# Reading each weight block in an order that alternates between its two halves: a float32r decoder layer on one core

## The chip, the core and the metric

The kernel runs on one core of a Trainium2 chip. The metric is the device time of one execution in microseconds (us); the time before is the median of 3 runs. The engines are named as in the profile: PE is TensorE (PEld its weight loads), DVE is VectorE, ACT is ScalarE, POOL is GpSimd, SP is SyncE, which here only issues DMAs.

## The reference

One layer of a decoder over 256 tokens of width 2048, in float32. Three attention branches of 4, 6 and 6 heads share one input projection; each branch is projected, gated and added; then an output projection with residual, and a SwiGLU feed-forward of width 5632 with residual.

```python
h = rmsnorm(x, g_mix)
proj = h @ w_in                      # 2048 -> 3*2048 (q, k, v) + 3*2048 (gates)
...
merged = (gates[:, :, 0] * (flat(o_a) @ w_branch[:ea])
          + gates[:, :, 1] * (flat(o_b) @ w_branch[ea:eb])
          + gates[:, :, 2] * (flat(o_c) @ w_branch[eb:]))
x = x + merged @ w_out
h2 = rmsnorm(x, g_ffn)
gu = h2 @ w_gu                       # 2048 -> 2*5632
x = x + (jax.nn.silu(gu[..., :D_FF]) * gu[..., D_FF:]) @ w_down
```

Nearly all the arithmetic is in the five matrices w_in, w_branch, w_out, w_gu and w_down.

## The kernel before

**Precision.** A float32 factor is kept as two float32r parts, high and low: `split` (line 104) lets ScalarE copy the value into a float32r tile (the high part) and VectorE subtract that from the value (the low part). A product of two such factors is three matmuls: high by high, high by low, low by high (`product`, lines 160 to 164). In each, a 128 x 128 piece of the activations (`h`, `hs`, `o`, `m`, `h2`, `a`) is the stationary operand, and a 128 x 512 piece of a weight is the moving one; the result goes to a 128 x 512 bank in PSUM.

**Tiling.** On the host, `by_blocks` (line 1083) lays each matrix out in blocks of 256 rows by 512 columns, so that one DMA of 512 KB brings a tile of 128 partitions x 2 x 512 words (`w_raw`, or `g_raw` where blocks are added to one another first). The tile is split into `w_hi` and `w_lo` (line 105), 128 x 1024 words in one instruction each, and every half of 512 is then the moving operand of products with both blocks of 128 tokens.

**Stages.** In order: the values, queries and keys, and gates from w_in, with the attention of earlier groups woven in by generators that advance a step after each weight block; the branch projections (w_branch) with the gates; the output projection (w_out); the feed-forward's first matrix (w_gu); its second (w_down). `project` (line 142) handles a group of 512 columns in the plain way. `project_pair` (line 320) and `down_pair` (line 974) take two groups at once, and for part of the rows use seven products in place of eight, with sums of activations and sums of weight blocks (`u`, lines 305 and 316). The first four row blocks of the first group go through an order written by hand (lines 500 to 506) beside the loading of x. All these ways end in the same matmuls of 128 x 512: lines 162, 163, 164, and 500, 503, 506.

**Other matmuls.** Transposes (line 184) and the attention (lines 632 to 712) use plain float32; eight matmuls on zeros (line 380) fill TensorE's time at the start.

**Order.** A scheduler sets the order of instructions on each engine, but for those that are pinned. SP issues all weight DMAs, into tiles of which 4 (`w_raw`) or 4 to 6 (`g_raw`) are there at a time; POOL issues the gates, the residual and the spilled activations.

Of the kernel before, what the change touches and what calls it, by code (L numbers as in the profile page):

```python
# [17 lines left out]
P = 128  # L18
# [10 lines left out]
NB = 512  # L29
# [25 lines left out]
def hybrid_block(ctx: ExitStack, tc: tile.TileContext, x, g_mix, w_in, q_gain, k_gain, w_branch, w_out,  # L55
                 g_ffn, w_gu, w_down, rel_bias, onehot, extra, out):
    nc = tc.nc
# [36 lines left out]
    def banks():  # L94

        turn.reverse()
        return [acc.tile([P, NB], F32, name=turn[1]) for _ in range(2)]
# [44 lines left out]
    def project(acts, k0, w, row0, nk, col0, ps=None, done=0, there=(), last=1):  # L142


        ps = ps or banks()
        held = []
        for k, w_hi, w_lo in weights(w, row0, done, nk, col0, there):
            if k:
                advance(stages)
            if k % 2 == 0 and k:  # L150
                advance(slow_stages)
            held.append((k, w_hi, w_lo))
            if k < nk - last or k == nk - 1:
                for t in range(NT):
                    for kk, hi, lo in held:
                        product(ps[t], *acts.plain(t, k0 + kk), hi, lo, kk == 0, kk == nk - 1)
                held = []
        return ps

    def product(ps, ah, al, wh, wl, start=False, stop=False):  # L160
        how = dict(skip_group_check=True)
        nc.tensor.matmul(ps, ah, wh, start=start, stop=False, **how)  # L162
        nc.tensor.matmul(ps, ah, wl, start=False, stop=False, **how)  # L163
        nc.tensor.matmul(ps, al, wh, start=False, stop=stop, **how)  # L164
# [155 lines left out]
    def project_pair(acts, w, colA, colB, begun=None, nxt=None):  # L320
# [7 lines left out]
        def form(ps, f, srcs, start, stop, split=False):  # L328
            for i, c in enumerate(acts.wc):
                wh, wl = srcs[i] if split else parts(srcs[i])  # L330
                for j in range(2):
                    product(ps, *acts.form(f, c, j), wh[:, j], wl[:, j], start and i + j == 0,
                            stop and i + j == len(acts.wc))

        def rest(n, k, p0, p1, start=False, stop=False):
            wh, wl = parts(load(w, k, cols[n]))
            for t, ps in ((1, p1), (0, p0)):
                for j in range(2):
                    product(ps, *acts.plain(t, k + j), wh[:, j], wl[:, j], bool(start and t == 1 and j == 0), stop and j == 1)
# [53 lines left out]
    h = Columns(p1, "h", KT)  # L393
# [58 lines left out]
    for k in (4, 6):  # L452
# [6 lines left out]
    columns = {c: [o_raw[:, 4 * i + 2 * t:4 * i + 2 * t + 2, :].rearrange("p h (a q) -> p (h a) q", a=2)  # L459
                   for t in range(NT)] for i, c in enumerate(WC)}  # L460
# [26 lines left out]
    ps0 = banks()  # L487
    his, los = ([wpool.tile([P, 2, NB], F32R, name=f"w_{n}") for _ in range(2)] for n in ("hi", "lo"))
    W_HI, W_LO = ([t[k // 2][:, k % 2] for k in range(4)] for t in (his, los))
    RAW = [raws[k // 2][:, k % 2] for k in range(4)]  # L490
    how = dict(skip_group_check=True, stop=False)
# [5 lines left out]
        nc.vector.tensor_sub(W_LO[k], RAW[k], W_HI[k].bitcast(F32))  # L497

    def high_high(t, k):
        nc.tensor.matmul(ps0[t], h.plain(t, k)[0], W_HI[k], start=k == 0, **how)  # L500

    def high_low(t, k):
        nc.tensor.matmul(ps0[t], h.plain(t, k)[0], W_LO[k], start=False, **how)

    def low_high(t, k):
        nc.tensor.matmul(ps0[t], h.plain(t, k)[1], W_HI[k], start=False, **how)

    with tc.manual_schedule(engines={mybir.EngineType.PE, mybir.EngineType.DVE, mybir.EngineType.Activation}):
        high(0)
        first_columns(0, 0, 2)  # L510
        first_columns(0, 2, 2)
        idle(3)
        high_high(0, 0)
        first_columns(1, 0, 4, False)
        low(0)
        high(1)
        high_high(0, 1)
        low_part(0)
        high_low(0, 0)
        low_high(0, 0)  # L520
        first_columns(1, 0, 4, True)
        low(1)
        low_high(0, 1)
        high_low(0, 1)
        turned = [transpose4(xs[1][0])]
        high_high(1, 0)
        high_high(1, 1)
        high_low(1, 0)
        high(2)
        low_part(1)  # L530
        high_low(1, 1)
        low_high(1, 0)
        low_high(1, 1)
        low(2)
# [412 lines left out]
    a = Chunks(None, "a", NF // 4, WD, False)  # L947
# [135 lines left out]
def by_blocks(w):  # L1083

    rows, columns = w.shape[1:]
    w = w[0].reshape(rows // (2 * P), 2, P, columns // NB, NB)
    return np.ascontiguousarray(w.transpose(3, 0, 2, 1, 4))


# [18 lines left out]
```

## Time and profile before

| | before |
|---|---|
| median of 3 runs | 1432.87 us (1432.37 to 1435.72) |
| span of the profiled execution | 1432.0 us |
| PE busy | 1422.3 us, 99%, 6404 matmuls |
| PEld busy | 1172.0 us, 82% |
| DVE busy | 1196.6 us, 84% |
| ACT busy | 881.7 us, 62% |
| moved by DMA | 310.09 MB, 217 GB/s |

The profile is one execution. Its span runs from the first to the last instruction; the median lies 0.9 us above it. A row of a group gives line, engine, operation, output <- inputs, shapes and count, then busy us and the mean ns of one, then the idle time of the engine before them and what ended it. Matmuls are pipelined, so their durations overlap, and the pace is the distance between starts. PEclk is the granted TensorE clock in tenths.

### The profile page before, as it was taken

The numbers are of one execution on the slowest core, as the hardware profiler recorded it, in microseconds if no ns is written. First come the engines' busy times: TensorE is split into PE (matmuls) and PEld (weight loads), VectorE is DVE, ScalarE is ACT, GpSimd is POOL, SyncE is SP. The second block draws the span as 40 slices with busy tenths as digits, with TensorE's granted clock in tenths as the row PEclk, the third lists the DMA queues.
The fourth block names the chain that finished last, engine by engine and source line by source line (L and its number), as shares of the span: only waits on it lengthen the run. The fifth ranks groups of instructions, "written<-read, shape, count | busy, mean of one in ns | idle before, by whom it ended". The sixth has DMA issues, their size and how long they took to land. (4 is left out here: it accounts for less than half of the span.)

```text
span 1432.0 us, 17773 instructions
## 1 busy us (share of the span) xinstructions
PE 1422.3 (99%) x6404; PEld 1172.0 (82%) x6404; DVE 1196.6 (84%) x1262; ACT 881.7 (62%) x1140; POOL 72.9 (5%) x133
## 2 busy tenths in 40 slices
PE   9999999999999999999999999999999999999998
PEld 7888888888888888888888888888888888788887
DVE  7888787857999887776689999999999998886775
ACT  7667876766766665444456666666666666554453
POOL 1000000000000002100100000000000010100000
PEclk9999999999999999999999999999999999999999
DMA  8763547464656758876786657566665666767552
GB/s 269 262 221 123 216 120 250 123 219 173 217 202 239 255 195 297 273 218 217 226 293 222 225 205 256 213 222 233 222 214 192 233 207 232 253 233 237 190 169 97
DMA packets 88168, 310.09 MB, mean 217 GB/s; under 512 B 10672, under 2 KB 12288, under 8 KB 88080
## 3 DMA queue, kind: packets, MB, share of 16 engines
q1 hardware_dynamic: 76896, 275.29, 56.1%
q0 software_dynamic: 10000, 32.62, 6.6%
q8 instruction: 50, 0.82, 0.2%
q10 hardware_dynamic: 1184, 1.06, 0.2%
q14 instruction: 38, 0.31, 0.1%
HBM read 292.65 MB, written 16.27 MB: 216 GB/s over the span
## 5 line engine op out<-in xcount | busy, mean ns | idle before, releaser
L105 DVE TENSOR_TENSOR w_lo<-w_raw,w_hi 128x1024 fp32r<-128x1024 f32 x334 | 406.3, 1222 | 90.8 <-ACT w_hi L105 87.3
L105 ACT CAST w_hi<-w_raw 128x1024 fp32r<-128x1024 f32 x334 | 349.2, 1052 | 165.2 <-PE qs L164 69.5
L105 ACT CAST w_hi<-g_raw 128x1024 fp32r<-128x1024 f32 x184 | 192.7, 1053 | 121.4 <-PE ps L164 41.2
L105 DVE TENSOR_TENSOR w_lo<-g_raw,w_hi 128x1024 fp32r<-128x1024 f32 x184 | 219.9, 1221 | 39.2 <-ACT w_hi L105 38.5
L105 ACT CAST w_hi<-u 128x1024 fp32r<-128x1024 f32 x138 | 145.1, 1054 | 136.0 <-DVE u L305 64.4
L105 DVE TENSOR_TENSOR w_lo<-u,w_hi 128x1024 fp32r<-128x1024 f32 x138 | 166.5, 1222 | 37.1 <-ACT w_hi L105 35.7
L163 PE MATMUL ps<-w_lo,h_hi 128*128 128x512 f32 x360 | 140.9, 391 | 0.0
L164 PE MATMUL ps<-w_hi,h_lo 128*128 128x512 f32 x360 | 140.5, 390 | 0.0
L162 PE MATMUL ps<-w_hi,h_hi 128*128 128x512 f32 x360 | 137.4, 392 | 0.0
L163 PE MATMUL qs<-w_lo,h_hi 128*128 128x512 f32 x332 | 129.9, 391 | 0.8 <-DVE w_lo L105 0.8
L164 PE MATMUL qs<-w_hi,h_lo 128*128 128x512 f32 x332 | 129.5, 390 | 0.0
L162 PE MATMUL qs<-w_hi,h_hi 128*128 128x512 f32 x332 | 126.6, 391 | 0.0
L305 DVE TENSOR_TENSOR u<-u,g_raw 128x1024 f32<-128x1024 f32 x80 | 94.4, 1219 | 0.0
L164 PEld LDWEIGHTS ps<-w_hi,h_lo 128*128 128x128 f32 x360 | 67.6, 188 | 14.3 <-DVE h_lo L105 0.3
L163 PEld LDWEIGHTS ps<-w_lo,h_hi 128*128 128x128 f32 x360 | 67.6, 188 | 13.6
L162 PEld LDWEIGHTS ps<-w_hi,h_hi 128*128 128x128 f32 x360 | 67.5, 188 | 13.7
L163 PEld LDWEIGHTS qs<-w_lo,h_hi 128*128 128x128 f32 x332 | 62.4, 188 | 13.9 <-DVE w_lo L105 1.2
L164 PEld LDWEIGHTS qs<-w_hi,h_lo 128*128 128x128 f32 x332 | 62.3, 188 | 13.5 <-issue 0.6
L162 PEld LDWEIGHTS qs<-w_hi,h_hi 128*128 128x128 f32 x332 | 62.3, 188 | 12.7
L316 DVE TENSOR_TENSOR u<-g_raw 128x1024 f32<-128x1024 f32 x40 | 48.8, 1220 | 17.5 <-DMA g_raw<-in_w_in 14.8
L162 PE MATMUL v<-w_hi,h_hi 128*128 128x512 f32 x120 | 47.5, 396 | 0.2 <-ACT w_hi L105 0.2
L305 DVE TENSOR_TENSOR g_raw<-g_raw 128x1024 f32<-128x1024 f32 x40 | 47.1, 1219 | 0.0
(397 smaller groups left out, 2934.6 us busy)
## 6 DMA issues: line engine op xcount, KB each, us to landing
w_raw<-in_w_in SPq DMA_DIRECT2D x118, 512.0 KB, 4.6
g_raw<-in_w_gu SPq DMA_DIRECT2D x88, 512.0 KB, 5.1
w_raw<-in_w_gu SPq DMA_DIRECT2D x88, 512.0 KB, 5.9
g_raw<-in_w_in SPq DMA_DIRECT2D x72, 512.0 KB, 5.6
w_raw<-in_w_down SPq DMA_DIRECT2D x64, 512.0 KB, 4.4
w_raw<-in_w_branch SPq DMA_DIRECT2D x32, 512.0 KB, 4.5
w_raw<-in_w_out SPq DMA_DIRECT2D x32, 512.0 KB, 4.1
g_raw<-in_w_down SPq DMA_DIRECT2D x24, 512.0 KB, 4.6
```

The costliest lines, as they stand in the source:

```text
L105: for op in nc.scalar.copy(hi, src), nc.vector.tensor_sub(lo, src, hi.bitcast(F32)):
L162: nc.tensor.matmul(ps, ah, wh, start=start, stop=False, **how)
L163: nc.tensor.matmul(ps, ah, wl, start=False, stop=False, **how)
L164: nc.tensor.matmul(ps, al, wh, start=False, stop=stop, **how)
L305: tc.keep_in_program_order(nc.vector.tensor_add(d, d, a))
L316: nc.vector.tensor_add(d, a, b)
```

## The change

The host lays out each row of 512 columns of a block with its 256 even columns first and its 256 odd columns behind them. The two parts of every weight tile keep that layout. Each matmul that reads such a part as its moving operand reads it through the view `woven`: for each b of 256, the word b of the first half, then the word b of the second. So the 512 results stand in PSUM in the natural order of the columns, as before. The sums of weight blocks are formed elementwise in the new layout. The lists of instructions of each engine, with shapes and order, are the same before and after.

```diff
+    def woven(w):
+
+        return w.rearrange("p (a b) -> p b a", a=2)
+
     def product(ps, ah, al, wh, wl, start=False, stop=False):
         how = dict(skip_group_check=True)
+        wh, wl = woven(wh), woven(wl)
         nc.tensor.matmul(ps, ah, wh, start=start, stop=False, **how)
         nc.tensor.matmul(ps, ah, wl, start=False, stop=False, **how)
         nc.tensor.matmul(ps, al, wh, start=False, stop=stop, **how)
...
     def high_high(t, k):
-        nc.tensor.matmul(ps0[t], h.plain(t, k)[0], W_HI[k], start=k == 0, **how)
+        nc.tensor.matmul(ps0[t], h.plain(t, k)[0], woven(W_HI[k]), start=k == 0, **how)
 
     def high_low(t, k):
-        nc.tensor.matmul(ps0[t], h.plain(t, k)[0], W_LO[k], start=False, **how)
+        nc.tensor.matmul(ps0[t], h.plain(t, k)[0], woven(W_LO[k]), start=False, **how)
 
     def low_high(t, k):
-        nc.tensor.matmul(ps0[t], h.plain(t, k)[1], W_HI[k], start=False, **how)
+        nc.tensor.matmul(ps0[t], h.plain(t, k)[1], woven(W_HI[k]), start=False, **how)
...
 def by_blocks(w):
 
     rows, columns = w.shape[1:]
-    w = w[0].reshape(rows // (2 * P), 2, P, columns // NB, NB)
-    return np.ascontiguousarray(w.transpose(3, 0, 2, 1, 4))
+    w = w[0].reshape(rows // (2 * P), 2, P, columns // NB, NB // 2, 2)
+    w = w.transpose(3, 0, 2, 1, 5, 4)
+    return np.ascontiguousarray(w).reshape(columns // NB, rows // (2 * P), P, 2, NB)
```

## The prediction

> **What bounds the kernel now.** I read first the busy shares and the slices with the clock, then who waits for whom on TensorE, then the order of time on TensorE in the middle of the output projection, and last the count of the products.
>
> ```profile
> span 1432.0 us, 17773 instructions
> PE 1422.3 (99%) x6404; PEld 1172.0 (82%) x6404; DVE 1196.6 (84%) x1262; ACT 881.7 (62%) x1140; POOL 72.9 (5%) x133
> PE   9999999999999999999999999999999999999998
> PEclk9999999999999999999999999999999999999999
> DMA  8763547464656758876786657566665666767552
> ```
>
> TensorE is busy in every slice at a granted clock of nine tenths or more, and all others have room: VectorE 84%, ScalarE 62%, the DMA engines some six tenths in most slices. Since matmuls overlap, 99% busy alone doesn't say that TensorE sets the pace; its list of waits does. Its columns are: who waited, for whom, microseconds in total, times, the longest.
>
> ```profile
> PE qs L163 <- DVE w_lo L105: 1.7, 4, 0.8
> PE tr L380 <- DVE sc L398: 1.5, 1, 1.5
> PE ps L162 <- ACT v L775: 0.6, 1, 0.6
> PE ps L503 <- DVE w_lo L497: 0.4, 1, 0.4
> ```
>
> These are the four longest; the other five are 0.2 to 0.4 us each. TensorE waits about 5 us of 1432 for anybody. So what one product takes on TensorE, times their number, is the time. The pace of a product stands in the timeline (start, duration, instruction): the durations overlap, and it is the distance of the starts that counts.
>
> ```profile
> 699.75 0.39 PE L162 MATMUL qs<-w_hi,m_hi 128*128 128x512 f32 x1
> 699.98 0.39 PE L163 MATMUL qs<-w_lo,m_hi 128*128 128x512 f32 x1
> 700.21 0.39 PE L164 MATMUL qs<-w_hi,m_lo 128*128 128x512 f32 x1
> ...
> 703.83 0.39 PE L162 MATMUL qs<-w_hi,m_hi 128*128 128x512 f32 x1
> ```
>
> From the first row to the last are 18 products (two starts every 0.45 us, the rows between left out): 4.08 us / 18 = 0.2267 us each. The counts, from the busy table of lines 162, 163 and 164 in turn over the whole span (length, busy time, count, clock, DMA share, GB/s), and from the groups of the hand-ordered start:
>
> ```profile
> 0.00:1432.00 1432.00, 745.21 (x1980) 1.00 0.63 217
> 0.00:1432.00 1432.00, 774.50 (x1980) 1.00 0.63 217
> 0.00:1432.00 1432.00, 770.97 (x1980) 1.00 0.63 217
> L500 PE MATMUL ps<-w_hi,h_hi 128*128 128x512 f32 x8 | 3.5, 463 | 0.0
> L506 PE MATMUL ps<-w_hi,h_lo 128*128 128x512 f32 x8 | 2.8, 394 | 0.0
> L503 PE MATMUL ps<-w_lo,h_hi 128*128 128x512 f32 x8 | 2.8, 407 | 0.4 <-DVE w_lo L497 0.4
> ```
>
> That makes 3 x 1980 + 3 x 8 = 5964 products, and 5964 x 0.2267 = 1352 us. The remaining 80 us of the span hold the 440 other matmuls (6404 - 5964: transposes and attention), the waits and both ends. All 5964 are changed.
>
> **The change part by part.** The edits outside TensorE touch these rows (a DMA issue with the KB of each and the us to landing; the splits and the transposes with busy time and mean ns):
>
> ```profile
> w_raw<-in_w_in SPq DMA_DIRECT2D x118, 512.0 KB, 4.6
> L105 ACT CAST w_hi<-w_raw 128x1024 fp32r<-128x1024 f32 x334 | 349.2, 1052 | 165.2 <-PE qs L164 69.5
> L105 DVE TENSOR_TENSOR w_lo<-w_raw,w_hi 128x1024 fp32r<-128x1024 f32 x334 | 406.3, 1222 | 90.8 <-ACT w_hi L105 87.3
> L184 PE MATMUL tr<-ident,sc 128*128 128x128 f32 x240 | 33.2, 272 | 0.1
> HBM read 292.65 MB, written 16.27 MB: 216 GB/s over the span
> ```
>
> *The layout in HBM.* The weights are reordered on the host within each row of 512, before the launch. The block that one DMA fetches is the same 128 x 2 x 512 words in one piece, so sizes and numbers of the DMAs stay. Cost nothing; nothing hides it because there is nothing.
>
> *The splits at line 105.* ScalarE's copy and VectorE's subtraction work on every word alike, in the order in which they lie: 1.05 and 1.22 us each, as before. Cost nothing.
>
> *Order, waits, PSUM.* No instruction is added, removed or moved on any engine, and no wait; a product's results go out in natural column order, so that everything behind reads what it did before. Cost nothing.
>
> *The read of the moving operand.* This is the whole change. Before, a product streams 512 four-byte words from neighbouring addresses. Now word 0, word 256, word 1, word 257 and so on: every step goes 1 KB forth or 1020 bytes back, and no two successive words are neighbours. The stationary operand (h, m, o, a) is read as before.
>
> No operation in the trace of before reads a moving operand in such an order, so I bound its price. Below: nothing. It can't be a gain, since 0.2267 us is also the pace of the fastest row of 512 columns, at full clock, with the neighbours already side by side. Above: the rows of slower streams. One slow stream at the full clock is the float32 (not float32r) matmul of the stick-breaking attention, which the profile shows as two passes of 128x512:
>
> ```profile
> 136.75 1.02 PE L652 MATMUL att<-pT,neg_after 128*128 128x512 f32 x2
> 137.61 0.61 PE L654 MATMUL att<-pT,neg_ones 128*128 128x128 f32 x4
> L652 PE MATMUL att<-pT,neg_after x4: 590/592/667, 136.7 to 166.5; 128*128 128x512 f32 x4
> L656 PE MATMUL att<-pT,neg_after x4: 379/380/382, 138.0 to 167.6; 128*128 128x256 f32 x4
> ```
>
> Its two passes take 137.61 - 136.75 = 0.86 us, so 0.43 each. The medians of 512 and 256 columns, 592 and 380 ns, differ by 212 ns: 0.83 ns a column, with 592 - 512 x 0.83 = 167 ns that don't depend on the columns. A product of the kernel, at 389 ns with the same fixed part, takes (389 - 167) / 512 = 0.43 ns a column. So TensorE has two paces in this trace at the same clock, one column in 0.43 ns and one in 0.83 ns, and the second is half the first. Still slower is the warm-up at the start, whose rows are also two to the product's one:
>
> ```profile
> 1.52 2.50 PE L380 MATMUL tr<-sc 128*128 128x512 f32 x5 [1.52 <-DVE sc L398]
> L380 PE MATMUL tr<-sc 128*128 128x512 f32 x8 | 4.1, 670 | 1.6 <-DVE sc L398 1.5
> L380 PE MATMUL tr<-sc x8: 628/628/797, 1.5 to 6.5; 128*128 128x512 f32 x8
> ```
>
> Five of them take 2.50 us, the last 0.63: (2.50 - 0.63) / 4 = 0.468 us each. And the slowest thing that the array does with a column is loading a weight, 128 of them in
>
> ```profile
> L162 PEld LDWEIGHTS ps<-w_hi,h_hi x360: 186/188/192, 15.7 to 1152.2; 128*128 128x128 f32 x180
> ```
>
> 188 / 128 = 1.47 ns a column, or 0.752 us for 512. That is the upper end of the price: 0.752 - 0.227 = 0.525 us a product; the lower end is 0.
>
> I take 0.43 us, the float32 pass. The supposition behind it: the product's pace of one word in 0.43 ns is held by fetching two neighbours at a time, which the woven order forbids, so that each fetch brings one useful word, and the pace is halved, to the one that the float32 pass shows. The weight load (0.188 us) stays hidden under 0.43 as it does under 0.227.
>
> The sum: 5964 x (0.430 - 0.2267) = 5964 x 0.2033 = 1212 us. Against it: the waits of TensorE on the splits, 5 us less the 1.5 at the very start, shrink, since VectorE and ScalarE then have twice the time for each block: 4 us. All other matmuls and both ends stay. The span becomes 1432.0 + 1212 - 4 = 2640 us. The median of the runs, 1432.87, lies 0.9 above the span of the profiled execution, so the forecast is 2641 us.
>
> [...]
>
> **The rivals.** *The address doesn't matter (not slower).* The place is the port that feeds the moving operand. [...] It decides as soon as the port gives a word each 0.2267 / 512 = 0.44 ns wherever it lies; also the case in which the read's pattern costs time that ends under the 0.188 us of the weight load and what follows it. For it speaks that the pattern is regular and short; against it, that 0.44 ns a word is the fastest stream in the whole trace (VectorE's 1222 ns for 1024 words is 1.2 ns), with the least time left for a fetch of its own. Chance 0.16.
>
> [...]
>
> *A part of it is hidden.* Fetches overlap so far that a column costs something between 0.43 and 0.83 ns. Halfway, 0.328 us a product: 1432 + 5964 x 0.1017 - 4 = 2035 us. For it: a queue of fetches ahead of the array would average over neighbours of the next step. Against it: the trace knows only the two paces, with nothing between, for 512 columns. Chance 0.12.
>
> *Each word costs more than two steps.* Successive words 1 KB apart could meet the same bank and wait for it. The bound is the weight load's 1.47 ns a column, 1432 + 5964 x 0.525 - 4 = 4559 us. Nothing in the profile speaks for it except that bound. Chance 0.11.
>
> **How the numbers follow.** Half the pace: 0.60. Within its own range, 0.424 us (512 x 212 / 256 ns) to 0.468 us (the warm-up) a product, it gives 1432 + 5964 x 0.1973 - 4 = 2605 to 1432 + 5964 x 0.241 = 2869 us. The address doesn't matter: 0.16. Part hidden: 0.12. More than two steps: 0.11. Faster: 0.01, for no reason that I can name. A measurement of this kernel tells about 0.3%, 4 us, from no change. Slower by more: 0.60 + 0.12 + 0.11 = 0.83; within it 0.16. The range leaves out only the case of more than two steps: from 1430, just under no change, to 2870, the upper end of half the pace.
>
> **What would show it right or wrong.** Right: starts of successive products at lines 162 to 164 some 0.43 us apart in every stage; durations near 592 instead of 389 ns; TensorE still 99% busy with waits under 5 us; VectorE at 1197 / 2640 = 45%, ScalarE at 33%, HBM traffic at 216 x 1432 / 2640 = 117 GB/s, each with the durations of single instructions unchanged; transposes at line 184 still 272 ns. Wrong: starts still 0.227 us apart (the first rival), between (the second), above 0.47 (the third); a granted clock under 1.00 in the slices, by which the pace would change for another reason; or LDWEIGHTS records longer than 188 ns.

## The result and the profile after

The changed kernel takes 1389.55 us (median of 4 runs, 1388.19 to 1391.12) against 1432.92 us (the kernel before, now also 4 runs): a ratio of 0.9693, 95% interval 0.9679 to 0.9707. The forecast was 2641 us. The woven read isn't slower than the plain one; each product is 11 ns faster.

The page of the kernel after, its span and busy line:

```profile
span 1387.4 us, 17773 instructions
PE 1364.3 (98%) x6404; PEld 1180.8 (85%) x6404; DVE 1190.5 (86%) x1262; ACT 879.0 (63%) x1140; POOL 72.6 (5%) x133
```

VectorE, ScalarE and GpSimd have the work they had. TensorE has the same 6404 matmuls in 58 us less. The timeline in the middle of the output projection (start, duration, instruction) shows where they went:

```profile
674.29 0.38 PE L169 MATMUL qs<-w_hi,m_lo 128*128 128x512 f32 x1
...
678.60 0.38 PE L168 MATMUL qs<-w_lo,m_hi 128*128 128x512 f32 x1
```

From the first row to the last are 20 products (the rows between left out): 4.31 / 20 = 0.2155 us (0.2158 over longer rows, below), where 0.2267 stood before. 5964 x 0.0108 = 64.4 us should have been gained; the span became only 44.6 us shorter. Most of the missing 20 us stand in the waits of TensorE, of which these are the longest (who waited for whom, us in total, times, the longest):

```profile
PE qs L168 <- DVE w_lo L105: 4.7, 7, 1.2
PE ps L168 <- DVE w_lo L105: 3.1, 6, 0.8
PE qs L167 <- ACT w_hi L105: 2.5, 4, 0.9
PE att L657 <- DVE rr L183: 1.8, 1, 1.8
```

The whole list adds up to 18.3 us, against 5.5 before, most of it for VectorE's and ScalarE's splits; some 3 us more are two short stretches at half the clock that follow such waits (last section). That leaves about 4 us that no view assigns. The table by stage says where the gain stayed behind. Its rows are w_in with the attention, w_branch, w_out, w_gu, w_down; the columns are start:end, length, then busy time (count) of PE, PEld, DVE, ACT and POOL, then clock, DMA share and GB/s. First before:

```profile
7.00:550.70 543.70, 540.96 (x2463) 444.75 (x2462) 456.17 (x514) 378.54 (x575) 18.52 (x32) 1.00 0.59 206
550.70:642.70 92.00, 92.00 (x420) 76.47 (x419) 66.01 (x77) 41.37 (x44) 15.06 (x28) 1.00 0.82 273
642.70:733.30 90.60, 90.60 (x418) 75.39 (x417) 61.16 (x71) 43.26 (x56) 6.50 (x12) 1.00 0.72 230
733.30:1194.60 461.30, 460.48 (x2069) 380.03 (x2068) 428.98 (x410) 297.17 (x340) 20.45 (x31) 1.00 0.63 224
1194.60:1432.00 237.40, 232.90 (x1029) 191.87 (x1027) 182.03 (x187) 118.87 (x122) 9.05 (x16) 1.00 0.62 200
```

and after:

```profile
7.20:530.50 523.30, 516.58 (x2463) 447.36 (x2462) 452.37 (x514) 376.77 (x574) 18.47 (x32) 1.00 0.61 213
530.50:618.10 87.60, 87.60 (x419) 76.91 (x418) 66.12 (x78) 41.54 (x44) 15.02 (x28) 1.00 0.84 288
618.10:704.50 86.40, 86.40 (x417) 75.90 (x417) 61.16 (x71) 43.50 (x56) 6.48 (x12) 1.00 0.77 242
704.50:1158.00 453.50, 445.15 (x2069) 384.33 (x2068) 426.44 (x410) 296.42 (x340) 20.39 (x31) 0.99 0.64 228
1158.00:1387.40 229.40, 223.30 (x1029) 192.72 (x1027) 181.83 (x188) 118.25 (x122) 9.01 (x16) 1.00 0.65 208
```

| stage | products | x 10.8 ns, us | measured, us |
|---|---|---|---|
| w_in | 2196 | 23.7 | 20.4 |
| w_branch | 384 | 4.1 | 4.4 |
| w_out | 384 | 4.1 | 4.2 |
| w_gu | 1980 | 21.4 | 7.8 |
| w_down | 1020 | 11.0 | 8.0 |

Where VectorE has room (75% and 71% in w_branch and w_out) the whole gain arrives. In w_gu VectorE was at 429 of 461 us before and is at 426 of 453.5 now, 94%: there 13.6 of the 20 us stay behind. Whether VectorE's work is the reason is what the runs with less of it ask, below. w_in and w_down, with VectorE at 86% and 79%, lose another 3 us each; for w_down, where that is 3.0 of 11.0, no run here asks why.

### The profile page after: what moved, and what is told of

It reads as the page before. It is cut to its first block, busy times and chain, and to the rows that moved or that the text cites. A ratio compares the mean times of both kernels' runs of the same rounds, so it can differ in the third digit from the quotient of the medians.

```text
span 1387.4 us, 17773 instructions
## 1 busy us (share of the span) xinstructions
PE 1364.3 (98%) x6404; PEld 1180.8 (85%) x6404; DVE 1190.5 (86%) x1262; ACT 879.0 (63%) x1140; POOL 72.6 (5%) x133
## 2 busy tenths in 40 slices
DMA packets 88168, 310.09 MB, mean 224 GB/s; under 512 B 10672, under 2 KB 12288, under 8 KB 88080
## 5 line engine op out<-in xcount | busy, mean ns | idle before, releaser
L105 DVE TENSOR_TENSOR w_lo<-g_raw,w_hi 128x1024 fp32r<-128x1024 f32 x184 | 217.9, 1219 | 23.7 <-ACT w_hi L105 23.2
L168 PE MATMUL ps<-w_lo,h_hi 128*128 128x512 f32 x360 | 137.1, 381 | 0.0
L169 PE MATMUL ps<-w_hi,h_lo 128*128 128x512 f32 x360 | 136.7, 380 | 0.2 <-DVE h_lo L105 0.2
L167 PE MATMUL ps<-w_hi,h_hi 128*128 128x512 f32 x360 | 133.5, 382 | 0.0
L168 PE MATMUL qs<-w_lo,h_hi 128*128 128x512 f32 x332 | 126.5, 381 | 1.2 <-DVE w_lo L105 1.2
L169 PE MATMUL qs<-w_hi,h_lo 128*128 128x512 f32 x332 | 126.0, 380 | 0.0
L167 PE MATMUL qs<-w_hi,h_hi 128*128 128x512 f32 x332 | 123.1, 381 | 0.0
```

The lines of the kernel that those rows point to most:

```text
L105: for op in nc.scalar.copy(hi, src), nc.vector.tensor_sub(lo, src, hi.bitcast(F32)):
```

## The experiments

**Ways of reading, TensorE alone.** Each row of the first ladder is 48 matmuls; their code differs in the view of the moving operand, and in some rows in the stationary operand, the length or the type (`step` reads every a-th word, `weave(w, a, c)` takes c words from each of a parts in turn):

```diff
+mm(ps[0], s, w, **how)                # line 55: plain
+mm(ps[0], s, weave(w, 2), **how)      # line 57: the woven read
+mm(ps[1], s, weave(w, 2, 2), **how)   # line 59: two words, then the other half
...
+mm(ps[1], s, step(w, 2), **how)       # line 75: every second word, then the others
...
```

> This kernel leaves the whole layer out: nothing of the reference is computed. It loads x, and TensorE alone runs rows of 48 float32r matmuls (fixed stationary tiles, one row per way of reading the moving operand), while every other engine and all DMAs rest. Pitch is the distance of starts. In the layer it was 226.7 ns for a plain read of 512 words and 215.7 for the woven one, 11 ns apart. Theory A, the plain read meets the weight load that runs beside it: plain stays 227 here; a stationary operand of 64 or 32 columns takes the 11 ns to about 5 or 3; 384 words cost the same 11 ns more than their woven read; a stationary operand read in steps changes the plain pitch. Theory B, the plain read loses something per word streamed: plain 227 with any stationary operand, the difference at 384 words is 8 ns; and among the runs (1, 2, 4, 8, 16, 64 words before the read changes halves) the 11 ns come back step by step as runs get longer. Theory C, a matter of the instruction's form (one run against two dimensions): every woven read, of whatever run, is at 216, and a start one or two words later changes nothing. Theory D, the 11 ns come from the other engines' or the DMAs' traffic in SBUF: plain is at 216 here. My prediction's supposition (each word a fetch of its own) has nothing left for the woven read; it would still make reads in steps of 4 or 8 words slow, about 430 ns.

Start of the row, its length, line, operands, count. One matmul takes the distance to the next row's start over 48:

```profile
21.03 11.04 PE L55 MATMUL acc<-mov,sta 128*128 128x512 f32 x48
31.91 10.52 PE L57 MATMUL acc<-mov,sta 128*128 128x512 f32 x48
42.27 16.48 PE L59 MATMUL acc<-mov,sta 128*128 128x512 f32 x48
58.58 12.18 PE L61 MATMUL acc<-mov,sta 128*128 128x512 f32 x48
...
162.40 21.83 PE L75 MATMUL acc<-mov,sta 128*128 128x512 f32 x48
184.05 22.26 PE L77 MATMUL acc<-mov,sta 128*128 128x512 f32 x48
...
237.89 11.28 PE L83 MATMUL acc<-mov,sta 128*32 128x512 f32 x48
249.01 10.52 PE L85 MATMUL acc<-mov,sta 128*32 128x512 f32 x48
259.37 8.50 PE L87 MATMUL acc<-mov,sta 128*128 128x384 f32 x48
267.70 7.96 PE L89 MATMUL acc<-mov,sta 128*128 128x384 f32 x48
275.50 5.91 PE L91 MATMUL acc<-mov,sta 128*128 128x256 f32 x48
281.25 5.52 PE L93 MATMUL acc<-mov,sta 128*128 128x256 f32 x48
286.61 11.38 PE L95 MATMUL acc<-mov,sta 128*128 128x512 f32 x48
...
309.24 11.44 PE L99 MATMUL acc<-mov,sta 128*128 128x512 f32 x48
320.52 11.57 PE L101 MATMUL acc<-mov,sta 128*128 128x512 f32 x48
331.94 10.53 PE L103 MATMUL acc<-movb,stab 128*128 128x512 bf16 x47
342.31 23.41 PE L105 MATMUL acc<-movb,stab 128*128 128x512 bf16 x48
```

| read (512 float32r words unless said) | line | ns |
|---|---|---|
| plain | 55 | 226.7 |
| woven, 1 word at a time | 57 | 215.8 |
| 2, 4, 8, 16, 64 words at a time | 59 to 67 | 340, 250, 243, 240, 227 |
| 4, 8, 64 parts in turn, 1 word each | 69, 71, 73 | 283, 488, 431 |
| steps of 2, 4, 8 words | 75, 77, 79 | 451, 460, 431 |
| plain, stationary of 64 columns | 81 | 230.4 |
| plain / woven, stationary of 32 columns | 83, 85 | 231.7 / 215.8 |
| plain / woven, stationary read in steps of 4 | 99, 101 | 235.0 / 237.9 |
| plain / woven, 384 words | 87, 89 | 173.5 / 162.5 |
| plain / woven, 256 words | 91, 93 | 119.8 / 111.7 |
| plain, starting 1 / 2 words late | 97, 95 | 238 / 233 |
| bfloat16 plain / woven / two at a time | 103, 105, 107 | 216 / 484 / 271 |

Both readings are there with every other engine at rest, so theory D falls. With a quarter of the stationary columns the difference grows to 15.9 ns (231.7 against 215.8) where theory A had 3: so it falls in the form in which it was put. The stationary operand isn't without influence, though: where it is read in steps of 4 words, both reads are slower, and the woven one (237.9) isn't faster than the plain one (235.0) any more. Reads of two dimensions are faster, slower or equal by their run (215.8, 340 and 227 ns with 1, 2 and 64 words at a time, against 226.7): theory C falls. It is 10.8 ns at 512 words and 11.0 at 384, where theory B had 8, so it isn't lost word by word, and theory B falls too: the plain read pays about 11 ns at both lengths. (At 256 words 8.1 ns are left. Matmuls of 128 words take 111 to 112 ns with either read in the second ladder, and the woven read of 256 words stands at the same 111.7, so there its time doesn't follow the number of words.)

The supposition of my prediction gives the time of reads by steps (451, 460 and 431 ns) and fails for the woven order. It doesn't give that of runs of two either: there each fetch of two neighbours would bring two useful words, which makes 227 ns, and they take 340. The woven float32r read and the plain bfloat16 read have the same pace (215.8 and 216.0 ns); the plain float32r read of this kernel doesn't reach it (226.7).

**The distance of the two words.** The second ladder keeps the alternation and changes how far apart its two words lie.

```diff
+def two(m, first, away, n=256, by=1):
+    w = m[:, first:first + 1]
+    return bass.AP(tensor=w.tensor, offset=w.offset, ap=[list(w.ap[0]), [by, n], [away, 2]])
...
+mm(ps[1], s, two(mov, k, 2), **how)     # line 58: 2 words away
+mm(ps[1], s, two(mov, k, 257), **how)   # line 74: 257 words away
...
+mm(ps[1], s, two(mov, k + 511, -256, by=-1), **how)  # line 98: backwards
...
```

> Leaves the whole layer out, like the first ladder: TensorE alone, rows of 48 float32r matmuls of 512 words. It changes the distance between the two words that are read in turn (2 to 1024 words instead of 256), the order of the halves, the direction, and the start of the read. [...] Theory F, it is a matter of banks: 216 only at some distances (256, and others of its multiples), and others such as 257, 258, 260 or 264 at 227 or more. [...]

```profile
30.98 10.52 PE L56 MATMUL acc<-mov,sta 128*128 128x512 f32 x48
41.34 10.56 PE L58 MATMUL acc<-mov,sta 128*128 128x512 f32 x48
...
124.25 10.52 PE L74 MATMUL acc<-mov,sta 128*128 128x512 f32 x48
...
248.61 10.52 PE L98 MATMUL acc<-mov,sta 128*128 128x512 f32 x48
258.97 11.29 PE L100 MATMUL acc<-mov,sta 128*128 128x512 f32 x48
```

All nineteen distances from 2 to 1024 words (lines 58 to 94), the halves swapped and the read backwards (line 98) run at 215.6 to 216.7 ns. Theory F falls: 257, 258, 260 and 264 words lie within 1 ns of 256. A woven read that starts 1 to 8 words late keeps 216 to 217; a plain one that starts 4 or 8 words late takes 232 or 233, and one that starts 64 or 256 words late 227 or 228. A row that alternates the two reads takes 224 ns each on average, between the two and above their middle (221). In all the rows with two words in turn, the words at even positions of the read are neighbours of one another, and so are those at odd positions. That isn't so in the other orders of the first ladder, and these are slower: 227 to 340 ns with runs of 2 to 64 words, 283 to 488 with 4 to 64 parts in turn, 431 to 460 in steps. But the plain read isn't of that kind either and loses only 11 ns, and with four parts in turn, as with two words at a time, successive words at even (or odd) positions are never neighbours, and yet the times are 283 and 340 ns. So this sorts the rows and doesn't give their times; what makes the woven order the fastest isn't shown.

**One stage alone.** The layout and the read are woven only for w_gu.

```diff
     def woven(w):
-        return w.rearrange("p (a b) -> p b a", a=2)
+        return w.rearrange("p (a b) -> p b a", a=2) if weaving[0] else w
...
+    weaving[0] = True
     for c in range(D_FF // NB):
...
+    weaving[0] = False
     WD = (4, 6, 8)
...
```

> Only the feed-forward's first matrix has the woven layout and read (11 column pairs of 180 products, 1980 of 5964); the others are laid out and read as before. If the gain is a fixed 11 ns at each woven product, starts of products are 216 ns apart in that stage and 227 in all others, and the time falls by 1980 x 11 = 22 us less the waits that grow there (12 us in that part of the changed kernel): 1432.9 to between 1411 and 1423 us. If the gain comes from elsewhere (the layout in HBM of all matrices, the order at the start), it isn't bound to that stage and the time falls by less than 5 or by more than 30 us.

Measured: 1425.92 us, ratio 0.9939 (0.9923 to 0.9956), so 8.6 us less. The stage's row and the next one:

```profile
732.30:1186.80 454.50, 445.02 (x2069) 384.44 (x2068) 426.33 (x410) 296.13 (x340) 20.44 (x31) 0.99 0.64 227
1186.80:1424.30 237.50, 232.99 (x1029) 191.88 (x1027) 182.28 (x188) 118.81 (x122) 9.05 (x16) 1.00 0.62 201
```

The stage is 6.8 us shorter, all others as before: the gain belongs to the products that are woven. The 8.6 us miss the expected 10 to 22: the waits and the clock take more of it than I allowed for (TensorE idles 9.5 us of the stage, 0.8 before; its granted clock there is 0.99, 1.00 before).

**Fewer additions on VectorE.** This kernel leaves out part of the sums of weight blocks in w_gu.

```diff
-        add_into(u, b22)
+        if w is not w_gu:
+            add_into(u, b22)
...
-        add_into(u, b21)
+        if w is not w_gu:
+            add_into(u, b21)
```

> The changed kernel, but in the feed-forward's first matrix the four additions of weight blocks to u per column pair (VectorE, 1.22 us each, 11 pairs, 54 us) are left out, so part of the sums of weights isn't formed there. If what the changed kernel doesn't gain in that stage (7.8 us shorter where 1980 x 11 ns are 21) is VectorE being the bound there, the stage falls from 453.5 to about 440 us, and the time from 1389.6 to 1373 to 1379. If the waits there come from ScalarE, the DMAs or the clock by itself, it stays within 3 us of 1389.6.

Measured: 1373.33 us, ratio 0.9586 (0.9570 to 0.9602). The stage w_gu:

```profile
706.10:1143.10 437.00, 437.00 (x2070) 383.02 (x2069) 380.74 (x366) 296.04 (x340) 20.56 (x31) 1.00 0.67 237
```

With 46 us less on VectorE, TensorE is busy for all of 437.0 us and waits for nobody. So these additions are what held back the gain there. Whether by VectorE's total load or by their place, the run can't tell: ScalarE's copy of `u` and the products of it wait right behind them, as around 755 us of the changed kernel (VectorE's addition, ScalarE's copy, TensorE's product, each with its idle time before it):

```profile
754.81 1.22 DVE L310 TENSOR_TENSOR u<-u,g_raw 128x1024 f32<-128x1024 f32 x1
755.00 1.04 ACT L105 CAST w_hi<-u 128x1024 fp32r<-128x1024 f32 x1 [2.50 <-DVE u L310]
756.10 0.48 PE L167 MATMUL ps<-w_hi,h_shi 128*128 128x512 f32 x1 [0.84 <-ACT w_hi L105]
```

**Two attempts to relieve VectorE with the whole computation kept.** The first uses the seven products for one row chunk of w_gu instead of two:

```diff
-        rest(1, ks[3], Z, V, stop=True)
+        for k in ks[3:]:
+            rest(1, k, Z, V, stop=k == ks[-1])
...
-    h2 = Chunks(pool(h2_stack, "h2p", "left"), "h", KT // 4, WC)
+    h2 = Chunks(pool(h2_stack, "h2p", "left"), "h", KT // 4, (0,))
...
-        if c in WC:
+        if c in h2.wc:
```

> The changed kernel, but in the feed-forward's first matrix only the first of the four row chunks goes through the seven products for eight, instead of two: 6 more matmuls per column pair on TensorE (11 x 6 x 0.216 = 14 us), 3 splits and 4 additions fewer on VectorE (11 x 7 x 1.22 = 94 us). If VectorE is the bound of that stage, TensorE becomes it: 11 x 186 matmuls x 0.216 = 442 us and some 11 us of transposes and evacuations, so the stage stays at about 450 us (453.5 now), and the time at 1384 to 1390. If VectorE isn't the bound, the stage gets 14 us longer: 1403 us.

Measured: 1404.08 us, ratio 0.9799 (0.9785 to 0.9814); the expectation of 1384 to 1390 missed, and the time is the 1403 us that it gave for the case that VectorE isn't the bound. The stage takes 467.9 us, though VectorE is down to 348: the added matmuls cost their 14 us, and TensorE's idle time (10.5 us, 8.4 in the changed kernel) doesn't shrink. TensorE's longest wait in it:

```profile
PE z L167 <- ACT sc L305: 4.9, 10, 0.5
```

Nearly once a pair, TensorE waits for ScalarE's copy of the bank z (line 305), a wait that the changed kernel doesn't have; other waits are for single splits. That the second chunk's products used to cover it is an argument, not shown. So less load on VectorE alone doesn't bring the gain back.

The second gives GpSimd the first additions:

```diff
-            nc.vector.tensor_add(d, a, b)
+            (nc.gpsimd if w is w_gu else nc.vector).tensor_add(d, a, b)
```

> The changed kernel, but the first two additions of weight blocks of each column pair in the feed-forward's first matrix (line 321, 22 in all) run on GpSimd, which is idle there, instead of VectorE (22 x 1.22 = 27 us of its 426 in that stage). If VectorE's work is the bound of that stage and GpSimd works beside it, the waits of 18 us there shrink and the time falls to 1376 to 1386 us. If the two engines hold each other up in SBUF (both read two operands there), or if GpSimd's addition is so slow that its u comes late, the stage doesn't get shorter: 1389 us or more.

Measured: 1412.64 us, ratio 0.9851 (0.9830 to 0.9872), beside 1389.11 for the changed kernel on the same chip: 1.7% slower than that.

> The changed kernel itself, for comparison with the next one on the same chip: 1389.6 us within 0.3%.

In the stage w_gu the additions, and VectorE's splits beside them, stand as

```profile
L321 POOL TENSOR_TENSOR u<-g_raw 128x1024 f32<-128x1024 f32 x20 | 83.0, 4168 | 205.8 <-DVE w_lo L105 205.8
L105 DVE TENSOR_TENSOR w_lo<-w_raw,w_hi 128x1024 fp32r<-128x1024 f32 x90 | 135.0, 1510 | 14.9 <-ACT w_hi L105 14.3
```

An addition takes 4.17 us in place of 1.22, and these splits of VectorE 1510 ns on average in place of 1219; the splits of `g_raw` blocks take 1362. VectorE's busy time in the stage rises from 426 to 446 us though it has fewer instructions. The granted clock of the stage is 0.98, 0.99 in the changed kernel. Why the splits are longer beside GpSimd's additions isn't shown, and how much of the loss comes from them, and how much from the later `u`, isn't separated. No version tried here beats the changed kernel with the whole computation kept.

**Two other orders in the whole layer.** The host's layout matches each:

```diff
-        return w.rearrange("p (a b) -> p b a", a=2)
+        return w.rearrange("p (a b c) -> p b a c", a=2, c=2)   # runs of two
...
+        return w.rearrange("p (b a) -> p a b", a=2)            # stepped
```

> The changed kernel, but two neighbouring words are read before the read changes halves (the host's layout to match). By the ladder's 340 ns for this read: 5964 x (340 - 226.7) = 676 us more than before less about 4 us of waits, 2105 us. If the layer hides part of it or the ladder doesn't hold beside other work, starts are less than 335 ns apart and the time under 2050 us. If the gain of the changed kernel came only from a read in two dimensions, this one would gain as well, about 1390 us.

> The host's layout is the inverse (even words of a row hold its first 256 columns, odd words the last 256), and every product reads all even words and then all odd ones, so the read goes forth by two words each time. By the first ladder's 451 ns for this read: 1432 + 5964 x (0.451 - 0.2267) - 4 = 2766 us. My prediction's supposition, half the pace wherever successive words are not neighbours, would give about 2641. [...] If the layer's other work mattered, it would be off by more than 3%.

Measured: 2067.43 us for runs of two (ratio 1.4431, 1.4402 to 1.4459) and 2761.82 for steps (1.9266, 1.9227 to 1.9304). In the stage w_out the starts of the first, then of the second, lie 0.33 and 0.45 us apart:

```profile
1000.16 0.51 PE L167 MATMUL qs<-w_hi,m_hi 128*128 128x512 f32 x1
1000.49 0.51 PE L168 MATMUL qs<-w_lo,m_hi 128*128 128x512 f32 x1
```

```profile
1299.81 0.63 PE L168 MATMUL ps<-w_lo,m_hi 128*128 128x512 f32 x1
1300.26 0.63 PE L169 MATMUL ps<-w_hi,m_lo 128*128 128x512 f32 x1
```

The stepped layer comes out 4 us from the 2766 that the ladder gave: with the pace of a product in hand, product count times pace is the time. Runs of two come out 38 us under the expectation, with 0.33 us a product in the rows above; why that is less than the ladder's 0.340 stays open.

## Why the prediction was wrong

- **What bounds the kernel** was right: TensorE's pace times 5964 products sets the time, and the two orders above confirm it to 0.2% and 2%.
- **Layout, splits, order, DMAs at no cost** was right: VectorE's and ScalarE's instructions kept their 1.22 and 1.05 us, and the DMAs moved the same 310.09 MB, at 224 instead of 217 GB/s in the shorter span.
- **"Below: nothing. It can't be a gain"** failed first. It took 0.2267 us for the array's own pace, because every product of the trace had it; the ladder shows 0.2158 for the woven read with nothing beside it, so the term of the sum that was taken as +0.2033 us a product measured -0.0108. The trace of before held a hint: the float32 pass costs 0.83 ns a column, and if a float32r column costs half of that, as the prediction has it, 512 of them make 212 ns, an estimate from these rows. The 14 ns above it could have been read as a cost that each plain product pays, and so one that another read might not pay. Instead "Faster" had a chance of 0.01 "for no reason that I can name", and the range, which is said to leave out only the case of more than two steps, leaves out this one too.
- **"the product's pace … is held by fetching two neighbours at a time, which the woven order forbids"** failed as the likeliest case. Reads by steps do cost about what I took, 0.43 (431 to 460 ns). But the price isn't due when the words alternate between two places, each read in order: 216 to 217 ns at nineteen distances. And runs of two, which keep two neighbours together, took 340 ns where the supposition gives 227. So the fetching of two neighbours doesn't explain the paces.
- **The upper end of "half the pace"**, 0.468 us from the warm-up, was probably no slower stream but the half clock: the product right behind the warm-up (line 500, at 6.96 us) takes 0.63 us as its rows do, products from 8.49 us on about 0.40, and in the stretch at clock 0.50 in the last section products take 0.63 and start 0.43 us apart. The row PEclk shows no drop there.
- **The first rival** came nearest, with no price where -10.8 ns a product was measured, but its reason isn't shown either: a port that gives a word each 0.44 ns "wherever it lies" would make steps as fast as the plain read, and they take 451 against 227 ns.
- **The waits of TensorE on the splits**, said to shrink by 4 us, had their sign from the slower pace. With the faster one the waits grew by 13 us by the list, and the loss is largest in w_gu, where VectorE needs 426 us.

What makes a plain float32r read pay 10.8 ns is left open. It is about the same at 512 and at 384 words and with every other engine at rest, and it changes with where the read starts (226.7 to 238 ns) and somewhat with the stationary operand (231.7 ns at 32 columns).

## What to carry to other kernels

Before calling a matmul's pace the array's own, compare it with columns times the time of a column from another row; a constant rest may be a cost that a different access pattern doesn't have (here 10.8 of 226.7 ns). For float32r moving operands of 512 words, two halves read in turn ran 4.8% faster than a plain read, but patterns close to it cost from nothing to 115% more (64 words at a time, eight parts in turn), and the same pattern more than doubled a bfloat16 matmul: measure the exact pattern and type in a ladder first. When the bounding engine gets 5% faster, look stage by stage for the next engine and for the chain through it: here the stage in which VectorE came to 94% kept back 13.6 of its 21.4 us.

## What the runs showed of the hardware beside that

Half the clock after short gaps. Around 800 us of the kernel after, TensorE waits twice for splits, 0.94 and 0.78 us, and the next seven starts lie 0.43 us apart instead of 0.216:

```profile
798.62 0.48 PE L167 MATMUL qs<-w_hi,h_shi 128*128 128x512 f32 x1 [0.94 <-ACT w_hi L105]
799.88 0.69 PE L168 MATMUL qs<-w_lo,h_shi 128*128 128x512 f32 x1 [0.78 <-DVE w_lo L105]
800.36 0.63 PE L169 MATMUL qs<-w_hi,h_slo 128*128 128x512 f32 x1
800.79 0.63 PE L167 MATMUL qs<-w_hi,h_shi 128*128 128x512 f32 x1
```

The table by windows gives the clock there (length, PE busy time, count, clock, DMA share, GB/s):

```profile
796.80:800.20 3.40, 1.68 (x7) 0.98 0.53 163
800.20:803.40 3.20, 3.20 (x9) 0.50 0.40 164
```

In 3.4 us TensorE was busy for 1.68, and the 3.2 us after it ran at half the clock, so the waits there cost up to another 1.6 us. The same happens once more at 885 us, after the same two waits of 0.94 and 0.78 us: the clock is 0.50 from 885.5 to 888.5 us. Not every such pair does it: after 0.84 and 0.78 us around 757 us (TensorE busy for 1.78 of 3.40 us) the clock stays at 1.00, and so it does after one wait of 1.80 us at 161 us (1.60 of 3.40 us busy). So what decides it isn't shown here.
